# Stick-breaking attention summed by parts: one sigmoid per score, a scan with a maximum, differences of values

## The chip, the cores and the metric

The kernel runs on one core of one Trainium2 chip. The metric is the device time of one execution in microseconds (us), median of three runs. A profiled execution is used to read where the time goes; its times are counted from the start of its span. The engines are named as in the profile: PE is TensorE's matrix products and PEld its weight loads, DVE is VectorE, ACT is ScalarE, POOL is GpSimd, SP is the engine that issues most transfers. A "q" behind a name means that engine's queue of transfers.

## What is computed

One layer of a streaming encoder over 1024 tokens of width 1024: a modulated norm, one input projection, attention in one branch and a gated convolution in the other, a merge, an output projection, and a feed-forward part. The change touches the attention (16 heads of 64 columns, blocks of 128 queries, each over all keys up to its own block's end) and the way its values reach it:

```python
def stick_breaking_attention(q, k, v):
    # A[t,s] = sigmoid(z_ts) * prod_{s<j<t} (1 - sigmoid(z_tj)),  z = q.k / sqrt(Dh), s < t
    for i in range(s_len // Q_BLOCK):
        t0 = i * Q_BLOCK
        n_keys = t0 + Q_BLOCK
        z = jnp.einsum('bhqd,bhkd->bhqk', qb, kp) * inv_sqrt
        mask = s_idx < t_idx
        log_not = jnp.where(mask, jax.nn.log_sigmoid(-z), 0.0)
        excl = lax.cumsum(log_not, axis=3, reverse=True) - log_not
        log_a = jax.nn.log_sigmoid(z) + excl
        a = jnp.where(mask, jnp.exp(log_a), 0.0)
        outs.append(jnp.einsum('bhqk,bhkd->bhqd', a, vp))
```

So each key's weight is its own sigmoid times the product of (1 - sigmoid) over all later keys before the query.

## The kernel before

All products run in a rounded 32-bit form (F32R). To keep accuracy, an operand is split into a high part (a ScalarE copy that rounds) and a low part (a VectorE subtraction of that copy from the original), and a product is made as high x high, high x low, low x high. Tiles rotate through buffers with a tag and a count ("bufs"). A planner places the instructions of each engine's queue by dependences and priorities with a model of their times; `tc.high_priority()`, `tc.issue_after()` and, in the first part, `in_order` steer it. Every queue then runs strictly in order.

The stages, by time in the profile: start and the first 512 columns of values (to about 95 us), keys with their norm, then the gates and queries by a Strassen scheme (to about 574), attention (585 to 1032), the rest.

**Values.** `finish_v` (L398 to L403) takes the projection's bank of 128 tokens x 512 columns, writes the high parts (L401, ScalarE) and low parts (L402, VectorE) side by side and stores them to `d_v`, which is laid out by head: [head, token in block, block, high 64 | low 64]. The first eight heads are made there, in the order of blocks 6, 7, 0, 1, ..., 5; the next product waits for the bank of the third of them. The other eight heads come from the first part of the filler (L824 to L846), with L843 and L844 doing the same.

**Attention.** A step is one head h and one block i of 128 queries; there are 128 steps, and step s means head s // 8 and block s % 8. `att_scores` (L725) makes the scores, 512 keys at a time, into one of two banks "z" (L737, L738) and takes two sigmoids from the bank: of the negated score into `pt` (L739) and of the score into `sg` (L740). `pt` is right-aligned in 1024 columns. A scan over it in reversed order (L744) forms the running product; `dm` adds 0 everywhere except on the diagonal of the last 128 columns, where the added 1 starts the product. L746 multiplies `sg` by the product shifted by one column. `att_trans` (L749), a step later, transposes the weights on PE, 128 x 128 each, into one of three banks "tr" (L760), and splits them (L763 on ScalarE, L764 on VectorE). `att_av` (L768), for two blocks at a time and three steps later, multiplies the value tile [high | low] of a head with the high and low weights (L775, L776) into the one bank "o", whose two halves of partitions are added (L779 copies one on ScalarE, L780 adds on VectorE) and stored.

**Loads.** `att_load` (L703) issues, on SP, six loads of queries and keys and one of the value tile `vt` for the next head (at the first step of each head). Each tag has two buffers.

**Filler.** Between the steps, a generator hands out other PE work: the second half of the values, the convolution branch (L819 to L821), and its projection. It has lower priority, and is dealt out in proportion to the attention's modelled work. Its SP loads and ScalarE-issued stores run through the same queues. When attention ends, its stored output is split into the buffers that attention leaves free (`slots`, L942) and multiplied by the branch's weights.

Of the kernel before, what the change touches and what calls it, by code (L numbers as in the profile page):

```python
# [28 lines left out]
def block_kernel(tc, x, x_t, cols, ada_1, ada_2, ada_row, w_q, w_kv, w_v1, w_cg, w_a, w_b, w_o, w_g, w_u, w_d, out):  # L29
# [8 lines left out]
    def nm(s):  # L38
        uid[0] += 1
        return f"{s}_{uid[0]}"  # L40
# [44 lines left out]
    ones = const.tile([P, P], F32, name="ones")  # L85
    nc.vector.memset(ones, 1.0)
    one = const.tile([P, 1], F32, name="one")
    nc.scalar.activation(one, ones[:, :1], AF.Sigmoid)
    sel0 = const.tile([P, 30], F32, name="sel0")
# [155 lines left out]
    for i in range(8):  # L245
        nc.tensor.matmul(warm, ones, xq[i][:, :512], start=True, stop=True)
# [150 lines left out]

    def finish_v(ps, i, ch):  # L398
        vs = ap.tile([P, 8, P], F32R, tag="vs", bufs=3, name=nm("vs"))
        pv = ps.rearrange("p (h d) -> p h d", d=DH)  # L400
        nc.scalar.activation(vs[:, :, :DH], pv, AF.Copy)  # L401
        nc.vector.tensor_tensor(out=vs[:, :, DH:], in0=pv, in1=vs[:, :, :DH].bitcast(F32), op=ALU.subtract)  # L402
# [12 lines left out]

    def more():
# [280 lines left out]

    NPT = 4
    pts = [ptp.tile([P, D + 1], F32, name=f"pt{j}") for j in range(NPT)]
    for pt in pts:  # L700
        nc.gpsimd.memset(pt[:, D:D + 1], 0.0)

    def att_load(h):  # L703
        pr, e0 = h // 2, (h % 2) * DH
        sqt = bp.tile([P, T], F32R, tag="sq", bufs=2, name=nm("sqt"))
        skh = bp.tile([P, T], F32R, tag="skh", bufs=2, name=nm("skh"))
        skl = bp.tile([P, T], F32R, tag="skl", bufs=2, name=nm("skl"))
        vt = bp.tile([P, KT, P], F32R, tag="vt", bufs=2, name=nm("vt"))
        for e in range(2):
            es = slice(e * DH, (e + 1) * DH)  # L710
            nc.sync.dma_start(sqt[es].bitcast(F32), d_q[e][pr, e0:e0 + DH, :])
            nc.sync.dma_start(skh[es].bitcast(F32), d_k[0][pr, e0:e0 + DH, :])
            nc.sync.dma_start(skl[es].bitcast(F32), d_k[1][pr, e0:e0 + DH, :])
        lastld[0] = nc.sync.dma_start(vt.bitcast(F32), d_v[h])
        hd[h] = (sqt, skh, skl, vt)

    hd = {}
    lastav = [None]
# [3 lines left out]
    ats = {}  # L722
    sgs = {}

    def att_scores(h, i):  # L725

        sqt, skh, skl, _ = hd[h]
        n = (i + 1) * P
        off = D - n
        npt[0] += 1  # L730
        pt = pts[npt[0] % NPT]
        sg = bp.tile([P, D], F32, tag="sg", bufs=NSG, name=nm("sg"))
        sgs[h, i] = sg
        for s0 in range(0, n, 512):
# [4 lines left out]
            nc.scalar.activation(pt[:, off + s0:off + s0 + m], z[:, :m], AF.Sigmoid, scale=rq[:, 1, i, h:h + 1])  # L739
            nc.scalar.activation(sg[:, s0:s0 + m], z[:, :m], AF.Sigmoid, scale=rq[:, 0, i, h:h + 1])  # L740
# [3 lines left out]
        nc.vector.tensor_tensor_scan(out=pt[:, rev], data0=pt[:, rev], data1=dm[:, rev], initial=0.0,  # L744
                                     op0=ALU.mult, op1=ALU.add)
        nc.vector.tensor_tensor(out=sg[:, :n], in0=sg[:, :n], in1=pt[:, off + 1:D + 1], op=ALU.mult)  # L746
        yield m / 512 * 0.43

    def att_trans(h, i):  # L749
        sg = sgs.pop((h, i))  # L750
        for b0 in range(0, i + 1, 4):
# [7 lines left out]
            for j in range(nb):  # L759
                nc.tensor.transpose(tr[:, j * P:(j + 1) * P], sg[:, (b0 + j) * P:(b0 + j + 1) * P], ident)  # L760
            c0 = (i % 2) * P
# [6 lines left out]
    def att_av(h, g):  # L768
        pr, e0 = h // 2, (h % 2) * DH
        vt = hd[h][3]  # L770
        o = pps.tile([P, 256], F32, tag="o", bufs=1, name=nm("o"))
# [6 lines left out]
        yv = bp.tile([DH, 256], F32, tag="oy", bufs=2, name=nm("oy"))  # L778
        nc.scalar.activation(tmp, o[DH:], AF.Copy)  # L779
        nc.vector.tensor_tensor(out=yv, in0=o[:DH], in1=tmp, op=ALU.add)  # L780
        hf, c0 = g // 2, (g % 2) * 256
# [3 lines left out]
    NZ, NTR, NPJ, DAV, KQ = 2, 3, 2, 3, 2  # L785
    NSG = 4
    LAST = (0, 1, 2, 3, 4, 5, 6, 7)
    ORDER = (0, 1, 2, 3, 4, 5, 6, 7)

    def attention():  # L790

        steps = [(h, i) for h in range(H) for i in (LAST if h == H - 1 else ORDER)]
        for s in range(len(steps) + DAV):
            if s < len(steps):
                h, i = steps[s]
                if s % 8 == (0 if h else 3) and h + 1 < H:
                    with tc.issue_after(lastld[0].ins):
                        att_load(h + 1)
                yield from att_scores(h, i)
            if 0 <= s - 1 < len(steps):  # L800
# [22 lines left out]
    def fillers():  # L823
        for e in range(2):  # L824
# [5 lines left out]
            for i in range(8):  # L830
                n, t0 = i // 4, (i % 4) * P
                ps = ps_f()[:, :256]
                for k in range(KT):
# [6 lines left out]
                    nc.tensor.matmul(ps, sl, wh, start=False, stop=(k == KT - 1))  # L840
                vs = fq.tile([P, 4, P], F32R, tag=("ybh", "ybl")[i % 2], bufs=2, name=nm("vs1"))
                pv = ps.rearrange("p (h d) -> p h d", d=DH)
                nc.scalar.activation(vs[:, :, :DH], pv, AF.Copy)  # L843
                nc.vector.tensor_tensor(out=vs[:, :, DH:], in0=pv, in1=vs[:, :, :DH].bitcast(F32), op=ALU.subtract)  # L844
                nc.scalar.dma_start(d_v[8 + 4 * e:12 + 4 * e, :, i, :].rearrange("h p d -> p h d"), vs.bitcast(F32))
                yield 1.3  # L846
# [56 lines left out]

    with tc.high_priority():
        att_load(0)
        for j in range(HEAD):
            next(fl)
# [20 lines left out]
    def preload_wo():  # L928

        for j in range(2):  # L930
# [3 lines left out]
            for k in range(2 - j):  # L934
# [6 lines left out]

    slots = [("skl", 2), ("sq", 2), ("skh", 2), ("vt", 2), ("skl", 2), ("sq", 2), ("skh", 2), ("sg", NSG), ("sg", NSG),  # L942
             ("sg", NSG), ("ath", 3), ("atl", 3), ("ath", 3), ("atl", 3), ("sg", NSG), ("vt", 2)]
    yah, yal = ([[None] * KT for n in range(2)] for e in range(2))
# [454 lines left out]
```

## Time and profile before

| | |
|---|---|
| median of 3 runs | 1887.13 us |
| lowest and highest | 1883.22, 1887.23 us |
| the profiled execution's own time | 1882.65 us |
| its span | 1880.9 us |
| mean granted TensorE clock | 0.993 |
| transfers | 360.05 MB, 191 GB/s over the span |

A row of grouped instructions gives the line, engine, operation, output <- inputs, shapes and count; behind the first bar the busy time (us) and the mean duration of one (ns); behind the second the engine's idle time just before them and what ended it. A row of the timeline gives start and length in us, then the instruction, and in brackets the idle time before it. A row of windows gives the stretch, its length, then the busy time and count for each engine, the granted clock, the transfers' share and GB/s. The page's rows of transfers end with the median time from issue to landing.

The page's second part shows the span in 40 slices (tenths of busy time); attention is slices 13 to 22:

```profile
PE   7899999999999999999998999979999999999999
PEld 5687778888878988877887888758888888878787
DVE  6774776778955999999998544599987888644954
ACT  4442553333345777777786211654444344332220
```

### The profile page before, as it was taken

What the parts mean: (1) busy time and instruction counts of PE and PEld (TensorE: products, weight loads), DVE (VectorE), ACT (ScalarE), POOL (GpSimd) and SP (SyncE); (2) the same over time, 40 slices, a digit from 0 to 9 for tenths busy, and PEclk for the clock granted to TensorE, in tenths of its full rate; (3) what the DMA queues carried; (4) which work ended last, traced back from release to release, by engine and by line L of the source; (5) the groups of instructions that cost most, each with busy time, mean ns of one, the idle gap of its engine ahead of it and who ended that gap; (6) DMA issues with size and microseconds to landing.
All of it is one profiled execution on the core that took longest, in us unless ns stands there. A gap on an engine that the chain in (4) does not pass through costs nothing.

```text
span 1880.9 us, 24952 instructions
## 1 busy us (share of the span) xinstructions
PE 1816.5 (97%) x8813; PEld 1507.0 (80%) x8813; DVE 1429.2 (76%) x2027; ACT 864.9 (46%) x1602; POOL 436.0 (23%) x317
## 2 busy tenths in 40 slices
PE   7899999999999999999998999979999999999999
PEld 5687778888878988877887888758888888878787
DVE  6774776778955999999998544599987888644954
ACT  4442553333345777777786211654444344332220
POOL 0043328324320000000000000255544454201013
PEclk9999999999999999999999999999999999999999
DMA  9699452227848666588654545314444344399666
GB/s 389 191 319 318 171 190 68 85 86 250 280 138 263 171 173 189 162 252 243 168 142 134 190 134 190 113 62 158 178 157 146 146 161 158 112 355 330 238 225 223
DMA packets 154764, 360.05 MB, mean 191 GB/s; under 512 B 15376, under 2 KB 52496, under 8 KB 152464
## 3 DMA queue, kind: packets, MB, share of 16 engines
q1 hardware_dynamic: 79792, 235.58, 39.3%
q10 hardware_dynamic: 73840, 119.22, 17.7%
q0 software_dynamic: 1008, 3.67, 0.5%
q8 instruction: 70, 1.15, 0.3%
q14 instruction: 54, 0.44, 0.1%
HBM read 243.58 MB, written 114.82 MB: 191 GB/s over the span
## 4 chain that ended last, share of the span: by engine, by line
PE 72%; DVE 15%; DMA 5%; ACT 4%; issue 2%; POOL 1%; ACTq 0%; SPq 0%; DVEq 0%; POOLq 0%
PE e L124 7%; PE e L125 7%; PE e L126 7%; PE pj L124 5%; PE pj L126 5%; PE pj L125 5%; PE pj L287 5%; PE pj L819 4%; PE pj L820 3%; PE pj L821 3%; PE e L1237 3%; PE e L1238 3%; PE e L1236 3%; DVE pt L744 3%; PE tr L760 2%
## 5 line engine op out<-in xcount | busy, mean ns | idle before, releaser
L744 DVE TENSOR_TENSOR_SCAN pt<-pt,dm 128x128 f32<-128x128 f32 (+7 forms) x128 | 171.5, 1344 | 6.0 <-ACT pt L739 5.5
L115 POOL TENSOR_SCALAR rs_m<-ss 128x1 f32<-128x1 f32 x8 | 1.7, 209 | 646.2 <-ACT xn L1069 646.2
L125 PE MATMUL e<-big,whi 128*128 128x512 f32 x352 | 138.1, 392 | 8.0 <-DVE big L129 8.0
L124 PE MATMUL e<-big,whi 128*128 128x512 f32 x352 | 137.8, 392 | 1.0 <-ACT c L1152 1.0
L126 PE MATMUL e<-big,wlo 128*128 128x512 f32 x352 | 137.5, 391 | 0.0
L739 ACT ACTIVATE pt<-z,rq 128x512 f32<-128x512 f32 (+1 forms) x192 | 112.7, 587 | 40.9 <-PE z L738 17.8
L1237 PE MATMUL e<-wlo,f 128*128 128x512 f32 (+1 forms) x319 | 122.9, 385 | 3.9 <-DVE wlo L1000 3.9
L124 PE MATMUL pj<-big,whi 128*128 128x512 f32 x320 | 125.1, 391 | 0.0
L125 PE MATMUL pj<-big,whi 128*128 128x512 f32 x320 | 124.7, 390 | 0.0
L126 PE MATMUL pj<-big,wlo 128*128 128x512 f32 x320 | 124.3, 390 | 0.0
L1238 PE MATMUL e<-whi,f 128*128 128x512 f32 (+1 forms) x319 | 122.6, 385 | 0.0
L129 POOL TENSOR_TENSOR ws<-raw,raw 128x512 f32<-128x512 f32 x41 | 60.0, 1464 | 263.1 <-DMA raw<-w_cg 120.0
L129 DVE TENSOR_TENSOR c<-e,c 128x512 f32<-128x512 f32 x154 | 103.1, 682 | 22.7 <-PE e L126 22.5
L1236 PE MATMUL e<-whi,f 128*128 128x512 f32 (+1 forms) x319 | 116.6, 383 | 2.2 <-DMA f<-d_f 1.7
L129 DVE TENSOR_TENSOR c<-pj,c 128x512 f32<-128x512 f32 x140 | 93.3, 682 | 30.9 <-PE pj L126 30.4
L287 PE MATMUL pj<-whi,big 128*128 128x512 f32 x352 | 110.5, 401 | 5.6 <-DVE vs L402 3.1
L740 ACT ACTIVATE sg<-z,rq 128x512 f32<-128x512 f32 (+1 forms) x192 | 112.7, 588 | 1.1 <-PE tr L760 1.1
L129 DVE TENSOR_TENSOR wlo<-raw,whi 128x512 fp32r<-128x512 f32 x116 | 87.0, 752 | 32.2 <-ACT whi L460 32.2
L460 ACT ACTIVATE whi<-raw 128x512 fp32r<-128x512 f32 x116 | 72.9, 633 | 83.7 <-PE pj L125 37.9
L764 DVE TENSOR_TENSOR atl<-tr,ath 128x512 fp32r<-128x512 f32 (+1 forms) x192 | 100.6, 543 | 5.8 <-ACT ath L763 3.3
L125 PE MATMUL e<-rl,whi 128*128 128x512 f32 x264 | 102.8, 389 | 1.7 <-DVE rl L129 1.7
L129 POOL TENSOR_TENSOR ws<-raw,ws 128x512 f32<-128x512 f32 x62 | 98.3, 1585 | 22.4 <-DVE wlo L1000 20.7
(246 smaller groups left out, 5240.7 us busy)
## 6 DMA issues: line engine op xcount, KB each, us to landing
f<-d_f SPq DMA_DIRECT2D x77, 512.0 KB, 4.4
d_f<-fs ACTq DMA_DIRECT2D x70, 512.0 KB, 2.6
raw<-w_cg SPq DMA_DIRECT2D x40, 512.0 KB, 4.0
raw<-w_g SPq DMA_DIRECT2D x24, 512.0 KB, 3.4
raw<-w_u SPq DMA_DIRECT2D x23, 512.0 KB, 3.3
ad<-ada ACTq DMA_DIRECT2D x19, 512.0 KB, 4.6
ada<-ada SPq DMA_DIRECT2D x8, 1024.0 KB, 10.0
d_t<-ts SPq DMA_DIRECT2D x16, 512.0 KB, 4.9
```

What stands on the lines that cost most here:

```text
L124: nc.tensor.matmul(ps, wh[:, k, :], fh[:, k, :], start=(k == 0), stop=False)
L125: nc.tensor.matmul(ps, wh[:, k, :], fl[:, k, :], start=False, stop=False)
L126: nc.tensor.matmul(ps, wl[:, k, :], fh[:, k, :], start=False, stop=(k == 3))
L129: eng.tensor_tensor(out=out, in0=a, in1=b, op=op)
L287: nc.tensor.matmul(ps, a, b, start=(k == 0 and q == 0), stop=(k == KT - 1 and q == 2))
L739: nc.scalar.activation(pt[:, off + s0:off + s0 + m], z[:, :m], AF.Sigmoid, scale=rq[:, 1, i, h:h + 1])
L740: nc.scalar.activation(sg[:, s0:s0 + m], z[:, :m], AF.Sigmoid, scale=rq[:, 0, i, h:h + 1])
L744: nc.vector.tensor_tensor_scan(out=pt[:, rev], data0=pt[:, rev], data1=dm[:, rev], initial=0.0, op0=ALU.mult, op1=ALU.add)
L764: nc.vector.tensor_tensor(out=tl[:, :nb, c0:c0 + P], in0=src, in1=th[:, :nb, c0:c0 + P].bitcast(F32), op=ALU.subtract)
L1236: nc.tensor.matmul(o, sh, w[0][:, c], start=(j == 0), stop=False)
L1237: nc.tensor.matmul(o, sh, w[1][:, c], start=False, stop=False)
L1238: nc.tensor.matmul(o, sl, w[0][:, c], start=False, stop=(j == NJ - 1))
```

## The change

Write C[s] for the product of (1 - sigmoid) over the keys s to t - 1 (1 for s at or beyond t). Then the weight of key s is C[s+1] - C[s], and the sum over a block with n keys can be taken by parts: the output is v[n-1] plus the sum over s of C[s] x (v[s-1] - v[s]), with v[-1] = 0. The changed kernel uses this:

- Only the sigmoid of the negated score is taken; `sg`, L740 and L746 go. `pt` itself is transposed. It has five buffers in place of four.
- The scan multiplies and then takes the maximum with a mask `mk` that is 1 on and above the diagonal of the last 128 columns and 0 elsewhere, starting from 1.
- Values are stored by token as plain 32-bit numbers in three arrays with a row of zeros ahead of the first token. `finish_v` makes one copy, on ScalarE and VectorE in turn, and the blocks run in their natural order.
- For each pair of heads, two loads fetch the values and the values shifted by one token (`va`, `vb`, one buffer each). `att_dv` subtracts them (once per pair) and splits the difference of a head into high and low.
- Each block's last value is added as a bias: `vlast`, made from a few rows by 16 small transposes in two parts, and two ScalarE operations of 128 columns with a bias in place of one of 256 without.
- The buffers in `slots` change: `va` and `vb` first, then more of `ath` and `atl` where `sg` was.

```diff
-    d_v = drp.tile([H, P, KT, P], F32, name="d_v")
+    d_v = [drp.tile([T + 1, n], F32, name=f"d_v{n}_{e}") for e, n in enumerate((512, 256, 256))]
...
-    dm = const.tile([P, D], F32, name="dm")
-    nc.gpsimd.memset(dm, 0.0)
-    ident = dm[:, D - P:]
+    ident = const.tile([P, P], F32, name="dm")
     make_identity(nc, ident)
+    mk = const.tile([P, D], F32, name="mk")
+    nc.gpsimd.memset(mk, 0.0)
+    nc.gpsimd.affine_select(out=mk[:, D - P:], in_=mk[:, D - P:], compare_op=ALU.is_ge, fill=1.0, base=-1,
+                            pattern=[[-1, P]], channel_multiplier=1)
...
-    def finish_v(ps, i, ch):
-        vs = ap.tile([P, 8, P], F32R, tag="vs", bufs=3, name=nm("vs"))
-        pv = ps.rearrange("p (h d) -> p h d", d=DH)
-        nc.scalar.activation(vs[:, :, :DH], pv, AF.Copy)
-        nc.vector.tensor_tensor(out=vs[:, :, DH:], in0=pv, in1=vs[:, :, :DH].bitcast(F32), op=ALU.subtract)
-        nc.scalar.dma_start(d_v[8 * ch:8 * ch + 8, :, i, :].rearrange("h p d -> p h d"), vs.bitcast(F32))
+    def finish_v(ps, i):
+        vs = ap.tile([P, 512], F32, tag=("vs", "qn")[i % 2], bufs=3 - i % 2, name=nm("vs"))
+        if i % 2:
+            nc.vector.tensor_copy(out=vs, in_=ps)
+        else:
+            nc.scalar.activation(vs, ps, AF.Copy)
+        nc.scalar.dma_start(d_v[0][1 + i * P:1 + (i + 1) * P], vs)
...
-    for i in (6, 7, 0, 1, 2, 3, 4, 5):
+    for i in range(8):
         mm_tok(pss[i], i, wq, 7, 8)
-        finish_v(pss[i], i, 0)
-        if i in (0, 2):
-            load_wq(6 + i // 2)
-            split_w(6 + i // 2)
+        finish_v(pss[i], i)
+        if i in (2, 4):
+            load_wq(5 + i // 2)
+            split_w(5 + i // 2)
     ends = in_order(i0)
+    for e in range(3):
+        nc.scalar.dma_start(d_v[e][0:1], mk[0:1, :d_v[e].shape[1]])
...
     def att_load(h):
...
-        lastld[0] = nc.sync.dma_start(vt.bitcast(F32), d_v[h])
+        if h % 2 == 0:
+            d, c0 = (d_v[0], pr * P) if h < 8 else (d_v[1 + (h - 8) // 4], pr % 2 * P)
+            va, vb = (bp.tile([P, KT, P], F32, tag=t_, bufs=1, name=nm(t_)) for t_ in ("va", "vb"))
+            for e, t in ((1, va), (0, vb)):
+                lastld[0] = nc.sync.dma_start(t, d[e:T + e, c0:c0 + P].rearrange("(i p) d -> p i d", p=P))
+            vab[:] = va, vb
+    def att_dv(h):
+        va, vb = vab
+        if h % 2 == 0:
+            tt(nc.vector, vb, vb, va, ALU.subtract)
+        dv = vb[:, :, h % 2 * DH:h % 2 * DH + DH]
+        vt = vts[h] = bp.tile([P, KT, P], F32R, tag="vt", bufs=2, name=nm("vt"))
+        nc.scalar.activation(vt[:, :, :DH], dv, AF.Copy)
+        tt(nc.vector, vt[:, :, DH:], dv, vt[:, :, :DH].bitcast(F32), ALU.subtract)
+    def load_vlast(e):
+        vl = bp.tile([8, 512], F32, tag="va", bufs=1, name=nm("vl"))
+        for d, c in (((0, 0),), ((1, 0), (2, 256)))[e]:
+            nc.sync.dma_start(vl[:, c:c + d_v[d].shape[1]], d_v[d][1:].rearrange("(i p) d -> i p d", p=P)[:, P - 1])
+        return vl
+    def turn_vlast(e, vl):
+        tr = pps.tile([P, 512], F32, tag="tr", bufs=NTR, name=nm("tr"))
+        for h in range(8):
+            nc.tensor.transpose(tr[:DH, h * 8:h * 8 + 8], vl[:, h * DH:(h + 1) * DH], ident[:8, :8])
+        nc.scalar.activation(vlast[:, 8 * e:8 * e + 8].rearrange("p h i -> p (h i)"), tr[:DH, :64], AF.Copy)
...
             nc.scalar.activation(pt[:, off + s0:off + s0 + m], z[:, :m], AF.Sigmoid, scale=rq[:, 1, i, h:h + 1])
-            nc.scalar.activation(sg[:, s0:s0 + m], z[:, :m], AF.Sigmoid, scale=rq[:, 0, i, h:h + 1])
...
-        nc.vector.tensor_tensor_scan(out=pt[:, rev], data0=pt[:, rev], data1=dm[:, rev], initial=0.0,
-                                     op0=ALU.mult, op1=ALU.add)
-        nc.vector.tensor_tensor(out=sg[:, :n], in0=sg[:, :n], in1=pt[:, off + 1:D + 1], op=ALU.mult)
+        nc.vector.tensor_tensor_scan(out=pt[:, rev], data0=pt[:, rev], data1=mk[:, rev], initial=1.0,
+                                     op0=ALU.mult, op1=ALU.max)
...
-                nc.tensor.transpose(tr[:, j * P:(j + 1) * P], sg[:, (b0 + j) * P:(b0 + j + 1) * P], ident)
+                nc.tensor.transpose(tr[:, j * P:(j + 1) * P], pt[:, off + (b0 + j) * P:off + (b0 + j + 1) * P], ident)
...
-        nc.scalar.activation(tmp, o[DH:], AF.Copy)
-        nc.vector.tensor_tensor(out=yv, in0=o[:DH], in1=tmp, op=ALU.add)
+        for e in range(2):
+            nc.scalar.activation(tmp[:, e * P:(e + 1) * P], o[:DH, e * P:(e + 1) * P], AF.Identity,
+                                 bias=vlast[:, h, 2 * g + e:2 * g + e + 1])
+        nc.vector.tensor_tensor(out=yv, in0=o[DH:], in1=tmp, op=ALU.add)
...
+                if s % 8 == 5 and h + 1 < H:
+                    att_dv(h + 1)
+                if s == 54:
+                    with tc.issue_after(lastld[0].ins):
+                        vl = load_vlast(1)
+                if s == 56:
+                    turn_vlast(1, vl)
                 yield from att_scores(h, i)
...
     with tc.high_priority():
+        vl = load_vlast(0)
+        turn_vlast(0, vl)
         att_load(0)
+        att_dv(0)
```

The filler's values (L841 to L845) are likewise copied once and stored plain.

More of the change, by code (lines that the diff above doesn't have):

```diff
@@ L696, in block_kernel @@
     bp = s3.enter_context(tc.tile_pool(name="phb", bufs=1, reuse_waits="tile"))
[L698 to L701, printed above, removed]
+    NPT = 5
+    pts = [ptp.tile([P, D], F32, name=f"pt{j}") for j in range(NPT)]
     def att_load(h):
@@ L713, in att_load @@
             nc.sync.dma_start(skl[es].bitcast(F32), d_k[1][pr, e0:e0 + DH, :])
-        lastld[0] = nc.sync.dma_start(vt.bitcast(F32), d_v[h])
-        hd[h] = (sqt, skh, skl, vt)
-    hd = {}
+        if h % 2 == 0:
[4 more added lines that the diff above has]
+            vab[:] = va, vb
+        hd[h] = (sqt, skh, skl)
+    def att_dv(h):
[16 more added lines that the diff above has]
+        nc.scalar.activation(vlast[:, 8 * e:8 * e + 8].rearrange("p h i -> p (h i)"), tr[:DH, :64], AF.Copy)
+    vlast = bp.tile([DH, H, 8], F32, name="vlast")
+    hd, vts, vab = {}, {}, []
     lastav = [None]
@@ L722, in block_kernel @@
     ats = {}
-    sgs = {}
+    ptof = {}
     def att_scores(h, i):
-        sqt, skh, skl, _ = hd[h]
+        sqt, skh, skl = hd[h]
         n = (i + 1) * P
@@ L840, in fillers @@
                     nc.tensor.matmul(ps, sl, wh, start=False, stop=(k == KT - 1))
[L841 to L845, printed above, removed]
+                vs = fq.tile([P, 256], F32, tag=("ybh", "ybl")[i % 2], bufs=2, name=nm("vs1"))
+                nc.scalar.activation(vs, ps, AF.Copy)
+                nc.scalar.dma_start(d_v[1 + e][1 + i * P:1 + (i + 1) * P], vs)
                 yield 1.3
```

20 lines of the change are left out of this document (8 added, 12 removed).

## The prediction

> **What bounds the kernel now.** I read the page's first part first, then cut the span into stages with the view by windows.
>
> ```profile
> PE 1816.5 (97%) x8813; PEld 1507.0 (80%) x8813; DVE 1429.2 (76%) x2027; ACT 864.9 (46%) x1602; POOL 436.0 (23%) x317
> ...
> 585.00:660.00 75.00, 72.90 (x560) 69.13 (x559) 67.87 (x103) 58.14 (x131) 0.00 (x0) 1.00 0.70 197
> 660.00:750.00 90.00, 86.88 (x519) 74.74 (x518) 88.02 (x129) 68.48 (x147) 0.00 (x0) 1.00 0.65 182
> 750.00:850.00 100.00, 95.35 (x562) 80.79 (x561) 96.87 (x145) 77.25 (x164) 0.00 (x0) 1.00 0.71 207
> 850.00:950.00 100.00, 96.92 (x582) 83.91 (x580) 95.55 (x139) 73.36 (x159) 0.00 (x0) 1.00 0.71 201
> 950.00:1032.00 82.00, 74.01 (x427) 63.99 (x426) 76.21 (x109) 58.58 (x122) 0.00 (x0) 0.96 0.45 133
> 1032.00:1100.00 68.00, 68.00 (x301) 56.10 (x300) 34.86 (x53) 18.13 (x30) 0.00 (x0) 1.00 0.52 170
> ```
>
> The columns after the length are PE, PEld, DVE, ACT and POOL busy time, granted clock, DMA share and GB/s. Attention fills 585 to 1032, 447.0 us. Summed over its five windows, PE is busy 426.1 us, VectorE 424.5 and ScalarE 335.8. Two engines are near their end together: VectorE at 98% in 660-750, PE at 95% over all. Where VectorE is light (1032-1100, 51%), PE loses nothing. So PE could go faster here; how much is read from the spacing of its starts.
>
> ```profile
> 684.42 0.39 PE L819 MATMUL pj<-big,whi 128*128 128x512 f32 x1
> 684.65 0.40 PE L820 MATMUL pj<-big,whi 128*128 128x512 f32 x1
> ...
> 686.25 0.82 PE L760 MATMUL tr<-dm,sg 128*128 128x128 f32 x6
> 686.83 0.36 PE L775 MATMUL o<-ath,vt 128*128 128x256 f32 x1
> 687.03 0.28 PE L776 MATMUL o<-atl,vt 128*128 128x256 f32 x1
> 687.15 0.28 PE L775 MATMUL o<-ath,vt 128*128 128x256 f32 x1
> ...
> 687.63 0.22 PE L775 MATMUL o<-ath,vt 128*128 128x128 f32 x1
> 687.69 0.27 PE L776 MATMUL o<-atl,vt 128*128 128x128 f32 x1
> ```
>
> Starts lie 0.23 us apart for 512 columns, 0.12 for 256, 0.06 for 128; six transposes take 0.58, about 0.10 each, with about 0.05 lost at each group's edge. **The floor of PE's work** follows: 742 products of 512 columns (L819 to L821) 170.7 us; 299 of 256 (L838 to L840) 35.9; the scores, 192 pairs of 128 to 512 columns, 66.9 (a 384 taken as 0.175); 576 transposes in 192 groups 67.2; the value products, 2 x (256 x 0.12 + 64 x 0.06) = 69.1. Together 409.8, so PE is not at work 37 us of 447. The page's idle time, 20.9, is smaller because each last matmul before a gap is drawn longer than its slot. What ends these gaps:
>
> ```profile
> L760 PE MATMUL tr<-dm,sg 128*128 128x128 f32 x576 | 91.8, 275 | 12.0 <-DVE atl L764 10.5 <-DVE sg L746 1.2
> L775 PE MATMUL o<-ath,vt 128*128 128x256 f32 x320 | 83.4, 285 | 1.6 <-DVE oy L780 1.6
> L737 PE MATMUL z<-skh,sqt 128*128 128x512 f32 (+1 forms) x192 | 71.9, 376 | 7.1 <-ACT sg L740 7.0
> ```
>
> Two thirds of it is VectorE behind on its queue (transposes find no free bank until L764 has read one), one third is the score bank, which the second sigmoid (L740) frees late. Both are what the change lightens.
>
> **VectorE, part by part.**
>
> ```profile
> L744 DVE TENSOR_TENSOR_SCAN pt<-pt,dm 128x128 f32<-128x128 f32 (+7 forms) x128 | 171.5, 1344 | 6.0 <-ACT pt L739 5.5
> L764 DVE TENSOR_TENSOR atl<-tr,ath 128x512 fp32r<-128x512 f32 (+1 forms) x192 | 100.6, 543 | 5.8 <-ACT ath L763 3.3 <-DMA skl<-d_k 2.1
> L746 DVE TENSOR_TENSOR sg<-sg,pt 128x128 f32<-128x128 f32 (+7 forms) x128 | 94.7, 746 | 4.3 <-ACT sg L740 0.6 <-ACT ath L763 0.5
> L844 DVE TENSOR_TENSOR vs<-pj,vs 128x256 fp32r<-128x256 f32 x13 | 5.3, 407 | 3.4 <-ACT vs L843 3.4
> ...
> L746 DVE TENSOR_TENSOR sg<-sg,pt 128x1024 f32<-128x1024 f32 x16 | 19.2, 1201 | 0.0
> L764 DVE TENSOR_TENSOR atl<-tr,ath 128x512 fp32r<-128x512 f32 x96 | 64.5, 677 | 2.5 <-ACT ath L763 2.4
> ```
>
> Gone are the 128 multiplications of L746 (94.7 us) and L844 (5.3 in this stage). Added are 8 differences of 1024 elements (1.2 each, by L746's widest form) and 16 low parts of 512 (0.68, by L764's): 9.6 + 10.9 = 20.5. The scan keeps its widths and operands' kinds, but its second operation becomes a maximum, which no row shows. The nearest row is L744 itself: 171.5. Below, it could be as cheap as L746's one pass (94.7); above, I bound it by both passes in a row (266.2). I take 171.5.
>
> [...]
>
> VectorE's load falls to 424.5 - 100.0 + 20.5 = 345 us, 81% of a stage of 425.
>
> **ScalarE.**
>
> ```profile
> L740 ACT ACTIVATE sg<-z,rq 128x512 f32<-128x512 f32 (+1 forms) x192 | 112.7, 588 | 1.1 <-PE tr L760 1.1
> L779 ACT ACTIVATE otmp<-o 64x256 f32<-64x256 f32 x64 | 24.5, 382 | 10.2 <-PE o L776 8.5 <-DVE vs L844 0.4
> L460 ACT ACTIVATE whi<-raw 128x512 fp32r<-128x512 f32 x38 | 24.3, 641 | 6.1 <-PE pj L820 5.5 <-PE pj L821 0.5
> L739 ACT ACTIVATE pt<-z,rq 128x128 f32<-128x128 f32 x32 | 12.3, 383 | 5.8 <-DMA skl<-d_k 3.2 <-PE z L738 1.1 <-DMA big<-d_yb 0.8
> ```
>
> L740 goes (112.7). Sixteen copies of 512 elements to the high part cost 16 x 0.64 = 10.2. The output's one copy becomes two of 128 columns with a column as bias; the nearest row is the sigmoid of 128 columns with a column as scale, 0.383, so 128 x 0.383 = 49.0 in place of 24.5. ScalarE falls to 335.8 - 112.7 + 10.2 + 24.5 = 258 us. The output bank is held some 0.4 us longer 64 times; between two groups lie two steps (447 / 128 = 3.5 us each), so this costs nothing unless the steps shrink to that.
>
> **PE** keeps all its products and gains 16 tiny transposes, about 0.1 each: 1.6 us on the path.
>
> **Queues and transfers.** Bytes loaded stay (16 x 512 KB); values arrive in runs of 512 bytes, as only the old stores wrote them.
>
> ```profile
> vt<-d_v SPq DMA_DIRECT2D x16, 512.0 KB, 4.6
> skl<-d_k SPq DMA_DIRECT2D x32, 256.0 KB, 6.7
> d_v<-vs ACTq DMA_DIRECT2D x8, 512.0 KB, 4.9
> ...
> 607.71 0.46 SPq L712 DMA_DIRECT2D skh<-d_k  x1
> 610.78 0.59 SPq L713 DMA_DIRECT2D skl<-d_k  x1
> ...
> 626.85 1.76 DVE L744 TENSOR_TENSOR_SCAN pt<-pt,dm 128x768 f32<-128x768 f32 x1
> ...
> 827.05 0.45 SPq L713 DMA_DIRECT2D skl<-d_k  x1
> 833.01 0.45 SPq L713 DMA_DIRECT2D skl<-d_k  x1
> 845.20 1.74 DVE L744 TENSOR_TENSOR_SCAN pt<-pt,dm 128x768 f32<-128x768 f32 x1
> ```
>
> The new wait is VectorE's: the difference for the next pair of heads stands in its queue ahead of the scan of the sixth block (768 columns), and everything on VectorE, then PE, waits behind it. For head 2 the six issues run from 607.71 to 611.4; two more of 0.6 end at 612.6, and the scan stands at 626.85: 14.2 us for a transfer whose nearest rows are 4.6 to 6.7. That is hidden. In the crowded stretch (head 10) the six issues end at 833.5, the two more at 834.7, and the scan is at 845.2: 10.5 us, still enough, but I charge 1 us. On SP, what stands behind the first value load is the weight load of the filler and the next head's keys; the first load also waits for eight transposes, which PE can do in the 10 us of filler ahead of attention. Nothing is charged. Three more row stores on ScalarE's queue and the mask's set-up on GpSimd lie beside idle time of those engines.
>
> **The projection of values at 73 us.**
>
> ```profile
> 76.30 0.69 DVE L402 TENSOR_TENSOR vs<-pj,vs 128x512 fp32r<-128x512 f32 x1 [1.09 <-ACT vs L401]
> ...
> 73.55 0.39 PE L287 MATMUL pj<-whi,big 128*128 128x512 f32 x1
> 77.04 0.50 PE L287 MATMUL pj<-whi,big 128*128 128x512 f32 x1 [3.11 <-DVE vs L402]
> ```
>
> PE stands from 73.8 to 77.04 until the third tile's low part is out of the bank it needs. Now that bank is the first tile's, emptied by one copy: 3.2 us are free. Starting earlier, PE reaches the fifth and seventh slice of the next weights sooner, whose split is late next; I give back 1.2, one low part of 1024 elements (L746's widest form), and keep 2.
>
> **The sum.** Of 37 us idle I let 15 remain: 5 of the 8.0 at the end of the stage (950-1032), where the last head's chain has no filler beside it; 4 where transfers hold ScalarE's or SP's queue; 6 in small gaps at group edges. Saved: 22, less 1.6 for PE and 1 for the wait, plus 2 at the values, about 21.5 to 22.5; I take 22. Against the profiled execution, 1882.65, this gives 1860.6. The runs' median is 1887.13, 4.5 above it, so I name 1865.
>
> **Rivals.**
> 1. *All the idle time goes.* With VectorE at 81% and a score bank freed after one sigmoid, PE runs at its floor: 37 - 1.6 + 2 = 37, hence 1850. For it: 1032-1100, PE full. Against it: the chain of the last head. 0.12.
> 2. *Deeper still*, if a matmul's slot is no floor: PEld is busy 372.6 us of the five windows, and a stage of that length gives 447 - 373 = 74 less, 1813. Against it: starts 0.23 apart with nothing between, and 1032-1100, where PE has no gap and PEld still shows 82%. 0.02. [...]
> 3. *Little comes through.* The gaps are put down to VectorE, but it was late because ScalarE stood behind transfers; then only the bank waits on L740 (7.0) and some 3 of the others go, with the 2 at the values, less 1.6 for PE: 10 less, 1877. For it: VectorE itself waited on a key load (2.1), and ScalarE too (3.2). 0.15.
> 4. *Slower: VectorE stands in front of the value loads.* Place: the difference ahead of the sixth block's scan, in 7 pairs (the first is before attention). Each pair costs landing less 14 us. To eat 22 us it needs 3.1 per pair, that is a landing of some 17 us, against 4.9 for stores in such runs; at 20 us it costs 7 x 6 = 42 - 22, hence 1907. 0.08.
> 5. *The scan with a maximum is dearer.* At the upper bound VectorE holds 345 + 95 = 440 us, at 97% a stage of 453: 6 slower, less 2, hence 1891. 0.04.
>
> The forecast itself has 0.59, with 14 to 30 us saved: 1857 to 1873. A difference of 0.2% (3.8 us) is about what a measurement of this kernel can tell from none. Faster: 0.59 + 0.12 + 0.02 and most of rival 3, 0.83. Same: the weak end of rivals 3 and 5, 0.05. Slower: 0.12. The range, 1849 to 1884, takes in rivals 1 and 3 and leaves out 2, 4 and 5.
>
> **What would show it.** Right: VectorE's busy time in attention near 345 us and ScalarE's near 258; the stage about 20 us shorter; PE's waits on L764 and on the sigmoid less than half; the scan's mean still 1344 ns; no gap of PE at 73 us. Wrong: the scan slower per element; VectorE idle in front of the difference, released by a DMA; PE's idle time unchanged with VectorE at 80%, which would be rival 3; first starts of attention later than 586.

## The result and the profile after

| | before | after |
|---|---|---|
| median (lowest to highest) | 1887.18 us (1879.1 to 1895.87), 12 runs | 1888.28 us (1886.03 to 1893.44), 12 runs |
| ratio to before, 95% interval | | 1.0011 [0.9995, 1.0027] |
| the profiled execution, its span | 1882.65, 1880.9 us | 1889.95, 1888.2 us |
| mean granted clock | 0.993 | 0.988 |

No change that can be told, where 22 us less was forecast. The page's first part and the view by windows of the kernel after, in the columns of the prediction (the windows are the same stretches):

```profile
PE 1823.1 (97%) x8829; PEld 1513.4 (80%) x8829; DVE 1363.6 (72%) x1903; ACT 792.9 (42%) x1488; POOL 438.6 (23%) x314
...
585.00:660.00 75.00, 71.00 (x535) 67.52 (x533) 55.53 (x73) 44.75 (x106) 0.00 (x0) 0.95 0.69 184
660.00:750.00 90.00, 88.47 (x523) 76.04 (x522) 76.50 (x107) 53.40 (x121) 0.00 (x0) 1.00 0.62 177
750.00:850.00 100.00, 90.00 (x528) 76.56 (x528) 78.40 (x109) 55.71 (x128) 0.00 (x0) 0.97 0.69 206
850.00:950.00 100.00, 94.78 (x549) 82.50 (x548) 80.36 (x109) 56.15 (x129) 0.00 (x0) 0.97 0.62 186
950.00:1032.00 82.00, 81.04 (x486) 70.06 (x484) 69.48 (x99) 49.40 (x113) 0.00 (x0) 1.00 0.45 130
```

VectorE fell from 424.5 to 360.3 us in these windows and ScalarE from 335.8 to 259.4: the load went. PE gained nothing from it: 425.3 us busy against 426.1, with fewer matmuls (x528 against x562 in 750-850), and the clock fell below 1 in three windows. The stage became longer in the profiled executions. Its first score and its last value product, before and then after, in the timeline of PE:

```profile
585.96 0.40 PE L737 MATMUL z<-skh,sqt 128*128 128x128 f32 x2
...
1030.53 0.41 PE L776 MATMUL o<-atl,vt 128*128 128x128 f32 x1
```

```profile
586.09 0.40 PE L772 MATMUL z<-skh,sqt 128*128 128x128 f32 x2
...
1038.39 0.28 PE L809 MATMUL o<-atl,vt 128*128 128x128 f32 x1
```

From start to start that is 444.6 us before and 452.3 after. The two profiled executions differ by 7.3 us in all, and all of it lies here; the medians differ by 1.1 only, since the profiled execution of before is 4.5 us below its median. The groups of the kernel after that answer to those shown of before:

```profile
L778 DVE TENSOR_TENSOR_SCAN pt<-pt,mk 128x128 f32<-128x128 f32 (+7 forms) x128 | 172.1, 1351 | 50.1 <-ACT pt L774 49.5
L774 ACT ACTIVATE pt<-z,rq 128x512 f32<-128x512 f32 (+1 forms) x192 | 107.7, 578 | 95.1 <-PE z L773 44.9 <-PE tr L793 24.7 <-DVE ybl L902 6.3
L793 PE MATMUL tr<-dm,pt 128*128 128x128 f32 x576 | 96.4, 277 | 9.9 <-DVE atl L797 7.8 <-DVE pt L778 1.8
L772 PE MATMUL z<-skh,sqt 128*128 128x512 f32 (+1 forms) x192 | 71.0, 372 | 10.3 <-ACT pt L774 10.3
```

VectorE now waits 49.5 us for sigmoids and ScalarE 44.9 for scores: each has time to spare. Yet PE still waits 7.8 us for low parts (10.5 before), and longer than before for the score bank (10.3 against 7.0). The view of waits over attention has what is new on VectorE, and on the queue of SP (time in all, times, longest):

```profile
DVE vb L132 <- DMA vb<-d_v: 22.9, 4, 18.6
DVE vb L132 <- DMA va<-d_v: 5.1, 1, 5.1
DVE vb L132 <- issue: 2.3, 1, 2.3
```

```profile
SPq L721 <- DVE vt L132: 26.7, 6, 7.2
```

VectorE stands in front of the value loads, and the load of `vb` stands too, until the odd head's difference has been read out of the one buffer. The timeline puts three of these places together; first a load of `vb`, then differences with the wait ahead of them:

```profile
654.39 0.38 SPq L721 DMA_DIRECT2D vb<-d_v  x1
...
592.37 1.23 DVE L132 TENSOR_TENSOR vb<-vb,va 128x1024 f32<-128x1024 f32 x1 [18.62 <-DMA vb<-d_v]
...
658.58 1.23 DVE L132 TENSOR_TENSOR vb<-vb,va 128x1024 f32<-128x1024 f32 x1 [1.11 <-DMA vb<-d_v]
...
785.16 1.23 DVE L132 TENSOR_TENSOR vb<-vb,va 128x1024 f32<-128x1024 f32 x1 [5.08 <-DMA va<-d_v]
```

The first pair's difference stands ahead of the first scan. The third pair's stands 4.2 us behind the issue of its load, ahead of head 2's widest scan (1024 columns, 659.73), where the program asks for it ahead of the sixth block of head 3 (768 columns, 678.35): the planner took it forward by 20 us.

PE's longest gap in the stage is another one. In the timeline of ScalarE and of PE:

```profile
842.50 0.69 ACT L774 ACTIVATE pt<-z,rq 128x512 f32<-128x512 f32 x1 [5.50 <-DMA d_ya<-oy]
```

```profile
843.24 0.47 PE L772 MATMUL z<-skh,sqt 128*128 128x128 f32 x1 [6.47 <-ACT pt L774]
...
844.26 0.63 PE L861 MATMUL pj<-big,whi 128*128 128x512 f32 x1
844.68 0.63 PE L862 MATMUL pj<-big,wlo 128*128 128x512 f32 x1
```

In the 5.50 us before 842.50 ScalarE computed nothing; what its queue did there was to issue two stores of the filler, at 840.53 (L903) and 842.12 (L904). PE then ran at about half speed (starts 0.42 us apart for 512 columns, where 0.23 is usual). Before had a stand at the same place, 3.25 us long:

```profile
840.68 0.37 ACT L739 ACTIVATE pt<-z,rq 128x128 f32<-128x128 f32 x1 [3.25 <-DMA skl<-d_k]
```

So three explanations stood: the relief is worth little (R); the value loads take it back (L), by VectorE's waits or by their traffic; ScalarE's stand at its own stores takes it back (Q). Theory V of the expectations is the wider form of L: the relief is real, and the new path of the values takes it back.

### The profile page after: what moved, and what is told of

It is laid out like the page before. It is cut to its first block, busy times and chain, and to the rows that moved or that the text cites. A ratio compares the mean times of both kernels' runs of the same rounds, so it can differ in the third digit from the quotient of the medians.

```text
span 1888.2 us, 24768 instructions
## 1 busy us (share of the span) xinstructions
PE 1823.1 (97%) x8829; PEld 1513.4 (80%) x8829; DVE 1363.6 (72%) x1903; ACT 792.9 (42%) x1488; POOL 438.6 (23%) x314
## 3 DMA queue, kind: packets, MB, share of 16 engines
q8 instruction: 70, 1.15, 0.2%
## 4 chain that ended last, share of the span: by engine, by line
PE 80%; DVE 9%; DMA 6%; ACT 2%; issue 2%; POOL 0%; ACTq 0%; SPq 0%; DVEq 0%; POOLq 0%
PE e L128 7%; PE e L129 7%; PE e L127 7%; PE pj L127 6%; PE pj L129 6%; PE pj L128 6%; PE pj L290 5%; PE pj L860 4%; PE pj L861 4%; PE pj L862 4%; PE e L1279 3%; PE e L1280 3%; PE e L1278 3%; PE tr L793 3%; PE o L809 2%; PE o L808 2%
## 5 line engine op out<-in xcount | busy, mean ns | idle before, releaser
L778 DVE TENSOR_TENSOR_SCAN pt<-pt,mk 128x128 f32<-128x128 f32 (+7 forms) x128 | 172.1, 1351 | 50.1 <-ACT pt L774 49.5
L774 ACT ACTIVATE pt<-z,rq 128x512 f32<-128x512 f32 (+1 forms) x192 | 107.7, 578 | 95.1 <-PE z L773 44.9
L127 PE MATMUL pj<-big,whi 128*128 128x512 f32 x320 | 125.2, 391 | 0.0
L128 PE MATMUL pj<-big,whi 128*128 128x512 f32 x320 | 124.7, 390 | 0.0
L132 DVE TENSOR_TENSOR c<-e,c 128x512 f32<-128x512 f32 x154 | 103.0, 683 | 21.4 <-PE e L129 21.4
L796 ACT ACTIVATE ath<-tr 128x512 fp32r<-128x512 f32 (+1 forms) x192 | 87.0, 489 | 49.7 <-PE o L808 30.2
L793 PE MATMUL tr<-dm,pt 128*128 128x128 f32 x576 | 96.4, 277 | 9.9 <-DVE atl L797 7.8
L860 PE MATMUL pj<-big,whi 128*128 128x512 f32 x256 | 104.7, 409 | 0.0
```

Source lines behind the costliest of these rows:

```text
L127: nc.tensor.matmul(ps, wh[:, k, :], fh[:, k, :], start=(k == 0), stop=False)
L128: nc.tensor.matmul(ps, wh[:, k, :], fl[:, k, :], start=False, stop=False)
L132: eng.tensor_tensor(out=out, in0=a, in1=b, op=op)
L793: nc.tensor.transpose(tr[:, j * P:(j + 1) * P], pt[:, off + (b0 + j) * P:off + (b0 + j + 1) * P], ident)
L860: nc.tensor.matmul(ps, wh, rh_, start=(k == 0), stop=False)
```

## The experiments

A ratio below is always to the kernel before on the same chip in the same set of runs; one thousandth is 1.9 us.

| run | median us | before | ratio, 95% interval |
|---|---|---|---|
| after | 1888.28 | 1887.18 | 1.0011 [0.9995, 1.0027] |
| e1 relief alone | 1874.39 | 1889.38 | 0.9926 [0.9901, 0.9951] |
| e4 after, load put back | 1922.25 | 1889.38 | 1.0183 [1.016, 1.0207] |
| e2 after, two `vb` | 1890.97 | 1889.38 | 1.0014 [0.9998, 1.0029] |
| e3 after, stores moved | 1880.03 | 1889.38 | 0.9953 [0.9938, 0.9969] |
| e5 before, stores moved | 1880.09 | 1887.31 | 0.9953 [0.9938, 0.9969] |
| e6 relief, stores moved | 1868.91 | 1887.31 | 0.99 [0.9883, 0.9918] |
| e7 e3 with one load | 1866.45 | 1887.31 | 0.9876 [0.9857, 0.9895] |
| e10 after with one load | 1874.95 | 1887.84 | 0.9927 [0.991, 0.9943] |
| e9 after, tied | 1877.48 | 1887.84 | 0.9946 [0.9927, 0.9965] |
| e12 after, first tied | 1891.06 | 1887.08 | 1.0015 [1.0001, 1.003] |
| e8 e3 tied | 1872.11 | 1887.31 | 0.9916 [0.99, 0.9932] |
| e11 e8 with four `oy` | 1869.69 | 1887.84 | 0.9899 [0.9881, 0.9918] |

**What the relief is worth (e1, e4).** In e1 the kernel before loses the second sigmoid and the multiplication (and has five buffers for `pt`); in e4 the kernel after gets as much load back.

```diff
-            nc.scalar.activation(sg[:, s0:s0 + m], z[:, :m], AF.Sigmoid, scale=rq[:, 0, i, h:h + 1])
...
-        nc.vector.tensor_tensor(out=sg[:, :n], in0=sg[:, :n], in1=pt[:, off + 1:D + 1], op=ALU.mult)
```

> The kernel before with only the weights' part of the change: the second sigmoid and the multiplication are left out and the scanned tile itself is transposed (so the weights are not the reference's); values by head, their loads and the scan with an addition stay. Theory V (the relief of VectorE and ScalarE is worth the predicted 20 us, and the new value path eats it): 16 to 24 us under the kernel before, PE not at work for some 15 us of attention. Theory Q (PE's gaps come from queues that stand behind transfers, so lighter engines only wait more): within 6 us of the kernel before, with PE's idle time as before and VectorE's load near 325 us.

```diff
+            nc.scalar.activation(pt[:, off + s0:off + s0 + m], z[:, :m], AF.Sigmoid, scale=rq[:, 1, i, h:h + 1])
...
+        tt(nc.vector, pt[:, off:], pt[:, off:], mk[:, off:], ALU.max)
```

The first added line is the kernel's own sigmoid a second time, the second a pass over the scan's result that changes nothing in it.

> The changed kernel with as much work put back as it took away: each sigmoid is taken twice into the same place, and behind each scan VectorE takes the maximum of the same columns with the mask once more (which changes no value). VectorE's load is then some 445 us. Theory V: 15 to 25 us slower than the changed kernel. Theory Q: 3 to 10 us slower, since only VectorE's bare load stands over the stage's length.

The relief alone took 0.74% off, 14 us; put back, it costs 1.0183 - 1.0011, 1.7% or 32 us. R falls: the load does cost, and what the change saves comes back elsewhere in it. That putting back costs more than twice what taking away saves need not contradict this: in the one case VectorE comes near its end again (415 us of 447 over the five windows of e4), in the other PE is near its own. That reading was not tested.

**Buffers (e2).** A second buffer for `vb`, and the first difference asked for at the third step:

```diff
-            va, vb = (bp.tile([P, KT, P], F32, tag=t_, bufs=1, name=nm(t_)) for t_ in ("va", "vb"))
+            va, vb = (bp.tile([P, KT, P], F32, tag=t_, bufs=b_, name=nm(t_)) for t_, b_ in (("va", 1), ("vb", 2)))
...
+                if s == 2:
+                    att_dv(0)
```

> The changed kernel with two buffers for vb (and four for pt), and the first pair's difference emitted at step 2 in place of ahead of the first scan. Theory V: VectorE's waits on value loads fall from 28 us to under 8, the gaps of PE at 594 to 604 and at 787 go with the drop of the clock behind them: 6 to 12 us under the changed kernel. Theory Q: at most 3 us under it.

No change, and the trace says why this doesn't test the waits: the planner put the first difference ahead of the first scan all the same, and the waits behind it still sum to 11.7 us (23.8 - 18.4 + 6.3), as in after. The timeline and the waits of e2:

```profile
592.10 1.23 DVE L132 TENSOR_TENSOR vb<-vb,va 128x1024 f32<-128x1024 f32 x1 [18.36 <-DMA vb<-d_v]
```

```profile
DVE vb L132 <- DMA vb<-d_v: 23.8, 3, 18.4
DVE vb L132 <- DMA va<-d_v: 6.3, 1, 6.3
```

**ScalarE's stores (e3, e5, e6).** The stores of the filler (`d_yb`, `d_mb`, the second half of `d_v`) are issued on GpSimd's queue; the same edit in after (e3), before (e5) and the relief alone (e6).

```diff
-            nc.scalar.dma_start(d_yb[0][n][:, m, :], yh.bitcast(F32))
+            nc.gpsimd.dma_start(d_yb[0][n][:, m, :], yh.bitcast(F32))
```

> The changed kernel with the filler's stores (yb, mb and the second half of the values) issued on GpSimd's queue in place of ScalarE's. Theory Q: ScalarE no longer stands behind them (5.5 us at 837, 3.9 at 866), the 6.7 us gap of PE at 843 and the low clock behind it go: 6 to 12 us under the changed kernel. Theory V: at most 3 us under it.

> The kernel before, whole, with one edit: the stores of the filler (yb, mb, the second half of the values) are issued on GpSimd's queue instead of ScalarE's. The same edit took 8 to 10 us off the kernel after (1888 to 1880 us). Theory Q1: ScalarE's stand at its own stores is a loss that both kernels have, and the change only kept it; then the kernel before gains about as much and ends at 1878 to 1882 us, a ratio of 0.995. Theory Q2: the change made the stand dear (the value loads fill the queue ahead of the attention's stores); then the kernel before gains little and ends at 1885 to 1890 us, a ratio of 0.998 to 1.001.

> The relief alone (the kernel before without the second sigmoid L740 and the multiplication L746, the scan's own result transposed, values by head as before; the weights are not the reference's) with the filler's stores on GpSimd's queue. The relief alone took 15 us off the kernel before (1874 us). If the stand at the stores and the relief are separate losses, they add up: 1864 to 1867 us, a ratio of 0.988. If it was the path of the values that made the stores dear, the store edit adds nothing here: 1872 to 1876 us. Against the kernel after with the same store edit (1880 us), what is left between the two is the price of the path of the values without the stores: 14 us by the first, 6 by the second.

It gains 0.58% in after (11 us), 0.47% in before (9 us) and 0.26% in the relief (5 us, with intervals that overlap; neither expectation for e6 was met). Q is a real loss, but before pays it about as well, so it doesn't tell the two apart: Q falls as the cause. In the trace of e3 the gap of 6.5 us at 843 is gone: VectorE, which in after waits 5.49 us for a sigmoid up to 843.22, waits at most 0.68 us at a time in 834-850 there.

**The value loads (e7, e10).** They are made for the first pair of heads alone, in e7 with the stores moved, in e10 on the kernel after itself.

```diff
-        if h % 2 == 0:
+        if h == 0:
             d, c0 = (d_v[0], pr * P) if h < 8 else (d_v[1 + (h - 8) // 4], pr % 2 * P)
...
-        if h % 2 == 0:
+        if h == 0:
             tt(nc.vector, vb, vb, va, ALU.subtract)
```

> The kernel after with the filler's stores on GpSimd's queue, and the two value loads and the difference made for the first pair of heads alone; all later heads take the first pair's difference (the weighted values are not the reference's). The copies and rounding differences of each head stay. If what is left of the price of the value path is the wait for the loads and their traffic (theory L), it comes to within 2 us of the relief with the same stores, 1866 to 1874 us, and the waits of VectorE for va at 784 us and of ScalarE for the landing of oy at 866 us go. If the loads after the first pair cost nothing, it stays at 1878 to 1881 us.

> The kernel after with one edit: the two value loads and the difference are made for the first pair of heads alone, later heads take the first pair's difference (the weighted values are not the reference's); the stores stay on ScalarE's queue. With the stores on GpSimd's queue the same edit took 13.5 us off (1880 to 1866.5 us), as far as the relief alone stands from after. If the loads after the first pair are the whole of what took the relief back, it ends as the relief alone did, 1872 to 1877 us, though VectorE still stands at the first pair's loads; if the store queue holds part of it, 1878 to 1884 us.

e10 ends where the relief alone does, 0.9927 against 0.9926: within the intervals, loads and differences after the first pair are the whole of what took the relief back, 1.0011 - 0.9927, 0.84% or 16 us. With the stores moved it is 0.77% (e3 to e7). L holds, and the stage shows it too: in the profiled execution of e10 it takes 436.2 us, 16.1 less than in after.

**Wait or traffic (e8, e9, e12).** The loads stay, and each difference is tied behind the latest scan at the place where the program asks for it; e9 on the kernel after, e8 with the stores moved, e12 for the first pair alone.

```diff
-        att_dv(0)
...
-                if s % 8 == 5 and h + 1 < H:
-                    att_dv(h + 1)
+                if s == 2 or s % 8 == 5 and h + 1 < H:
+                    with tc.issue_after(lastsc[0].ins):
+                        att_dv(h + 1 if s > 2 else 0)
```

> The kernel after with the filler's stores on GpSimd's queue, and each head's difference of values tied behind the latest scan at the place where the program asks for it, the first one behind the second scan instead of ahead of the attention; all loads as in after, the output the reference's. If the price is VectorE standing at a difference that was placed ahead of its data (place, not traffic), the waits for vb before the second scan and for va at 784 us go, and it ends at 1873 to 1877 us. If the price is the loads' traffic, or these waits are covered, it stays at 1878 to 1881 us.

> The kernel after with one edit: each head's difference of values tied behind the latest scan, the first one behind the second scan instead of ahead of the attention; the filler's stores stay on ScalarE's queue. The same edit took 8 us off where the stores were on GpSimd's queue (1880 to 1872 us). Theory P (the place of the difference is a loss of its own): 1878 to 1882 us, a ratio of 0.994 to 0.997, and VectorE no longer stands at vb ahead of the first scan. Rival: with the stores on ScalarE's queue its stand there covers the gain, and it stays at 1885 to 1889 us with the stand near 840 us as long as in after (5 us and more).

> The kernel after with the first pair's difference alone tied behind the second scan; the differences of the other seven pairs stay where after has them. All eight tied took 10 us off against the kernel before (1877.5 us, where after itself stood at 1888). Counted from the waits of VectorE in after: the first difference holds the first scan back from 588.2 (all tied) to 593.5 us, 5.3 us; the other seven waits sum to 11.7 us. If both count as they are long, this run ends between the two, 1883 to 1886 us, a ratio of 0.997 to 0.999. If the first alone is the price: 1877 to 1880 us. If the later ones alone are: 1887 to 1890 us.

e9 takes 0.65% off the kernel after, 12 of the 16 us; its stage takes 440.6 us, 11.7 less than in after. Its third difference now stands 19 us behind its load instead of 4, and no wait is listed in front of it. The view of waits has one left on VectorE in front of the loads, at the first pair. The timeline and the waits of e9:

```profile
652.99 0.38 SPq L721 DMA_DIRECT2D vb<-d_v  x1
...
672.14 1.20 DVE L132 TENSOR_TENSOR vb<-vb,va 128x1024 f32<-128x1024 f32 x1
...
1027.31 0.28 PE L810 MATMUL o<-atl,vt 128*128 128x128 f32 x1
```

```profile
DVE vb L132 <- DMA vb<-d_v: 2.6, 1, 2.6
```

e12 separates the first pair's wait from the others: of VectorE's wait of 18.6 us ahead of the first scan it leaves 1.8 (behind that scan, at 590.18), and it gained nothing. Of those 18.6 us VectorE had no other work for most of the time: in e12 it waits 13.8 us at the same place for the first sigmoid. Its start, all its waits in front of differences and its last value product:

```profile
587.33 1.06 DVE L779 TENSOR_TENSOR_SCAN pt<-pt,mk 128x128 f32<-128x128 f32 x2 [13.83 <-ACT pt L775]
590.18 1.23 DVE L132 TENSOR_TENSOR vb<-vb,va 128x1024 f32<-128x1024 f32 x1 [1.79 <-DMA vb<-d_v]
```

```profile
DVE vb L132 <- DMA vb<-d_v: 6.1, 4, 2.5
DVE vb L132 <- DMA va<-d_v: 5.1, 1, 5.1
DVE vb L132 <- issue: 2.4, 1, 2.4
```

```profile
1038.20 0.28 PE L810 MATMUL o<-atl,vt 128*128 128x128 f32 x1
```

So it is the short waits that come with the loss: five with 11.8 us (13.6 less the first pair's 1.8) in front of later pairs, which e9 removes, and there the stage ends at 1027.3 in place of 1038.2. The expectation that both count by their length was wrong. What isn't separated: the tie also changes the order around the difference. Of PE's larger gaps in after, one (787.17, 2.51 us for the low part behind the difference of 785.16) follows directly on such a wait; those at 872 and 905 vanish in e9 as well without following on one. How much of the 12 us is the standing and how much the changed order stays open, and so does the remainder to e10 (0.9946 against 0.9927, with intervals that overlap), which traffic could take, or the seven differences of 1.2 us each that e10 leaves out as well. With the stores moved this remainder is clear of noise: the tie gains 0.37% there (e3 to e8, 7 us), about half of the 0.77%, and e8 and e7 (0.9916 and 0.9876) have intervals that don't overlap. So the place of the differences isn't the whole price.

**A faster version (e11).** e8 with four buffers for the stored sums:

```diff
-        yv = bp.tile([DH, 256], F32, tag="oy", bufs=2, name=nm("oy"))
+        yv = bp.tile([DH, 256], F32, tag="oy", bufs=4, name=nm("oy"))
```

> The kernel after with the stores on GpSimd's queue and the differences tied behind the scans (1872 us), and four buffers in place of two for oy, the sum of a pair of row blocks that is stored to d_ya. In that run VectorE waited 4.7 us near 863 us for a store of oy to land. If the two buffers cost what PE stands there, it gains 1 to 3 us (1869 to 1871 us); if the time is spent elsewhere, it stays at 1871 to 1873 us.

By their ratios e8 is 16 us and e11 19 us faster than before, with the whole computation kept. That the buffers are worth the difference of the two isn't shown, as the intervals overlap. With the relief kept and the waits out of VectorE's queue, four of the five windows of attention in e11 look thus:

```profile
585.00:660.00 75.00, 74.36 (x575) 71.33 (x575) 64.70 (x86) 50.07 (x118) 7.05 (x13) 1.00 0.76 203
660.00:750.00 90.00, 89.76 (x532) 77.65 (x531) 76.97 (x108) 54.22 (x125) 8.67 (x16) 1.00 0.60 177
750.00:850.00 100.00, 98.45 (x589) 84.32 (x588) 87.39 (x120) 60.81 (x139) 9.21 (x17) 1.00 0.78 238
850.00:950.00 100.00, 97.99 (x583) 84.67 (x582) 85.45 (x117) 60.21 (x140) 4.78 (x9) 1.00 0.67 180
```

PE is at work 360.6 of these 365 us, 344.3 in after and 352.1 in before, and the clock is full throughout.

## Why the prediction was wrong, step by step

- **The new wait, charged at 1 us: this is the step that failed.** With the loads that it waits for it costs 12 to 16 us (e9, e10). Two premises were wrong. The difference was taken to stand where the program asks for it, ahead of the sixth block's scan; the planner moved it ahead, to 4.2 us behind the issue. And the two value loads were taken to be issued together, right behind the keys; but `vb` has one buffer, its load waits on SP until the odd head has been split (26.7 us in six waits), and so it is issued late: for the third pair at 654.39, where `va` had gone out at 611.07. The longest wait behind the first, 5.08 us and the only one for `va`, has a third source, which the prediction put at nothing: the rows for `vlast` of the last eight heads (`vl`, L739, issued at 720.49) hold `va`'s one buffer until PE has transposed them (L745, the last from 777.91), and the load of `va` goes out at 778.34, 6.8 us ahead of its difference. Landing itself was a little above the 4.6 to 6.7 assumed, in the rows of transfers for attention:

```profile
va<-d_v SPq DMA_DIRECT2D x8, 512.0 KB, 6.8
vb<-d_v SPq DMA_DIRECT2D x8, 512.0 KB, 7.3
```

- **Rival 4** named this mechanism, VectorE in front of the value loads, at the wrong price: it asked for 3.1 us of standing per pair to eat the gain. In after VectorE stood 11.7 us beside the first pair (22.9 - 18.6 + 5.1 + 2.3), 1.7 per pair, and that came with the loss of a gain that was itself smaller than forecast.
- **The relief, 22 us: mis-sized.** Alone it measured 14 us (e1, 9 to 19 by the interval). Its profiled execution, 1880.32 us, is the longest of its five runs. There the stage, from the first score (591.05) to the last value product (1025.45), takes 434.4 us, 10.2 less than in before; by the prediction's floor of 409.8 that leaves 24.6 us idle in place of 15, an estimate, since the filler's share of the stage may differ. In the same trace attention starts 5.1 us later than in before (591.05 against 585.96; e6 has 591.96), in a part that the edit doesn't touch. Why stays open, and with it how much of the missing 8 us lies ahead of the stage. Two allowances came near: PE's idle time in 950-1032 is 5.0 us, as allowed for the tail, most of it in the gap below; and moving the stores gains 5 (e6), where 4 was allowed for transfers that hold a queue.

```profile
1022.47 0.39 PE L772 MATMUL o<-ath,vt 128*128 128x256 f32 x1 [3.38 <-DVE oy L777]
```

- **The sum** itself has a slip without weight: its terms, 22 - 1.6 - 1 + 2, make 21.4 and not 21.5 to 22.5.
- **The scan with a maximum** costs what the one with an addition did, 1351 against 1344 ns. Rival 5 is out. In the trace of after one scan of 1024 columns took 2.28 us (at 659.73), and one difference of as many 1.23 (at 658.58).
- **ScalarE's load** was right: 259.4 us against 258. **VectorE's** came out at 360 instead of 345. By groups it fell by 84 us (462 to 378), against 79.5 worked out; but the durations listed for neighbours overlap (the difference at 658.58 is listed with 1.23 us, and the scan behind it starts 1.15 later, at 659.73), and the busy time of the windows counts an overlap once, so an operation that overlaps its neighbours frees less than its listed time.
- **The values at 73 us**: the stall went, and its gain did not arrive. The windows of before, then of after:

```profile
70.00:95.00 25.00, 21.89 (x97) 17.81 (x96) 15.85 (x22) 11.74 (x17) 0.00 (x0) 1.00 0.96 287
...
480.00:520.00 40.00, 39.98 (x175) 32.50 (x173) 38.50 (x60) 13.10 (x22) 14.76 (x8) 1.00 0.84 287
```

```profile
70.00:95.00 25.00, 25.00 (x112) 20.71 (x111) 18.51 (x27) 9.91 (x13) 2.82 (x3) 1.00 0.85 307
...
480.00:520.00 40.00, 37.80 (x165) 30.46 (x164) 37.89 (x61) 12.70 (x21) 11.38 (x7) 1.00 0.76 272
```

  Of the 3.1 us gained, 2.2 are given back in 480-520, and attention starts at the same time (586.09 against 585.96). The 2 us of this term were 0; where the rest went isn't shown.
- **Rival 2** found no support: over the four windows of e11 PE is at work 99% of the time while PEld shows 87%, as 1032-1100 of before had it (full, 82%).
- **Rival 3**, gaps that are queues behind transfers, was right about a real loss (the stores), but it holds in both kernels and explains nothing of their difference.
- **The signs named beforehand** would have told this: VectorE idle in front of the difference, released by a DMA, and PE's idle time unchanged (20.9 us before, 21.7 after in the five windows), were both listed under "wrong", the second as a sign of rival 3.

## What to carry to other kernels

Where a planner orders the queues, read the place of a new waiting instruction from the order that it made, not from the program, and tie it behind work that must not wait. Count for each new load which buffer it needs and who frees that last; a single buffer can turn an early load into a late one (here `vb`'s went out at 654.39, `va`'s of the same pair at 611.07). Judge a wait by what stands behind it in the queue: here one of 18.6 us ahead of the first scan cost nothing that could be measured, since there was little to do behind it yet, and five with some 12 us between them, in the full stretch that follows, went with a loss of 12.

## What the runs showed of the hardware

Some gaps of PE cost more than their length here: behind the one to 843.24 starts for 512 columns lay 0.42 us apart in place of 0.23, at a granted clock of 0.50. Windows of 2 us around two gaps of the kernel after (to 843.24, and to 905.53, the latter 2.73 us long by its row):

```profile
838.00:840.00 2.00, 0.00 (x0) 0.00 (x0) 0.00 (x0) 0.00 (x0) 0.00 (x0) 1.00 1.14 204
840.00:842.00 2.00, 0.00 (x0) 0.00 (x0) 0.00 (x0) 0.00 (x0) 0.00 (x0) 0.69 1.10 384
...
844.00:846.00 2.00, 2.00 (x6) 1.52 (x6) 1.97 (x4) 0.64 (x3) 0.00 (x0) 0.50 1.04 415
...
906.00:908.00 2.00, 2.00 (x11) 1.79 (x9) 1.09 (x2) 0.95 (x2) 0.00 (x0) 0.50 1.04 405
```

The granted clock falls to 0.50, with PE at work again from 843.24, and is back at 1.00 in 848-850; behind the second gap it is 0.74 in 908-910. The gap to 843 was 6.47 us long and the one to 905 shorter, and both were followed by half clock; so was one of 1.80 us to 593.98 (0.75 in 594-596, 0.50 in 596-598, which holds a second gap of 1.28), while the one of 2.51 us to 787.17 was not (1.00 in 786-788 and in 788-790). Length alone doesn't tell these four apart; what does isn't shown.
